# A two-block transformer on one core: first modulation's products written ahead of the norm, rope tables and gates behind the first dense block

## The chip, the cores and the metric

The kernel runs on one core of a Trainium2 chip. The metric is the device time of one execution in microseconds; three executions of the kernel before are given, and one more was taken with a profile.

## What is computed

`reference()` runs two blocks over 256 tokens of width 1024, all in fp32. The change lies in the opening of the first block:

```python
def first_block(x, c, positions, w_ada, b_ada, norm1_g, w_in, b_gate, conv_w, ...):
    mod = jax.nn.silu(c) @ w_ada[l] + b_ada[l]          # 1024 -> 6 * 1024
    sh1, sc1, g1, sh2, sc2, g2 = jnp.split(mod, 6, axis=-1)
    h = rms_norm(x, norm1_g[l]) * (1.0 + sc1[:, None, :]) + sh1[:, None, :]
    proj = h @ w_in[l]
    q_a, k_a, v_a, qk_m, v_m, o_m, gates = jnp.split(proj, offs, axis=-1)
    # rope on q_a, k_a and block attention; a causal convolution of width 4 and silu on qk_m;
    # a chunkwise mLSTM whose input and forget gates come from `gates`
    ...
    # output projection, second modulated norm, mixture of 32 experts, residual
```

Behind it come the mixture of experts and a second block (gated linear attention, a state space layer, attention to a memory), which the change does not touch.

## The kernel before, in words

Activations are kept transposed, 128 partitions of the width by 256 tokens, eight slices `k`. A product with a weight is made from two halves of each operand, `hi` and `lo`, by three matmuls (`mm3`, L282 to L286). Weights come in tiles `w` of 1 MB by SyncE's queue (`load`, L254), through a pool of five buffers. `halves` (L271) takes such a tile in two halves of 1024 columns: ScalarE copies each to `whi` (L267), VectorE subtracts to get `wlo` (L268). A dense block of 256 output columns (`dense_t`, L288) is two column tiles, one per half; for each it runs 8 slices by 3 matmuls, so 48 matmuls of 128x256 in all.

`first` (L437) sets the order of the work around the change; the scheduler lets instructions of one engine pass each other only as its priorities and the data allow, and the order on each engine is fixed before the kernel runs.

- The norm: `rstd` (L352) squares eight slices on ScalarE (L324, tile `ats`, two buffers) and sums each by two matmuls with one column (`ps<-c_ident,ats`); a square root and a reciprocal (L333, L334) give `cvc`, two matmuls spread it over the partitions and ScalarE copies it to `cv` (L349). VectorE scales the input with it (L448).
- Rope tables: the positions come by DMA (L450), and VectorE and ScalarE make sine and cosine (L463 to L465, `sincos` L360). The mask constants and the frequencies come by `load_c` (L444), `c_cmask` being one transfer.
- The modulation: `ada` (L404) loads eight 1 MB slices of `wada`, multiplies each with the replicated condition `crep` in four matmuls of 32x512, copies the sum (`ats`, L414), transposes it (L417) and adds a bias (`mod`, L420). The generator yields after each slice. The first third is run through at L467; the other two are kept in `more`, and one step of it is taken behind each later dense block (`next(more)`).
- `hh` and `hl`: the scaled input, modulated, as `hi` on ScalarE (L474) and `lo` on VectorE (L475, L476), slice by slice.
- Gates: `wg` and `bg` come by DMA, eight matmuls make `ml<-s,wg`, and `gates` (L570) takes a sigmoid and a logarithm on ScalarE, running sums on VectorE, transposes (L598) and products that spread them (L280, `ml<-s,c_cmask`).
- Dense blocks: four of them, b = 0, 2, 1, 3 (L488), each followed by one `more` step, a copy to `raw` (L493) and the convolution (L498 to L500).

Of the kernel before, what the change touches and what calls it, by code (L numbers as in the profile page):

```python
# [13 lines left out]
I32 = mybir.dt.int32  # L14
U8 = mybir.dt.uint8
AF = mybir.ActivationFunctionType
OP = mybir.AluOpType
AX = mybir.AxisListType

T = 256  # L20
# [187 lines left out]
class Kern:  # L208
# [86 lines left out]
    def steps_t(self, ps, src, act):  # L295
        for c, w in enumerate(self.halves(src)):
            w = [x.rearrange("p (k m) -> p k m", k=8) for x in w]
            for k in range(8):
                self.mm3(ps[:, c], [x[:, k] for x in w], [x[:, k] for x in act], k == 0, k == 7)
                if k % 4 == 3:  # L300
                    yield

    def dense_n(self, src, act):

        ps = self.psum().rearrange("p (a b) -> p a b", a=2)
        for _ in self.steps_n(ps, src, act):
            pass
        return ps
# [128 lines left out]
    def first(self, M):  # L437
        nc, io, tc = self.nc, self.io, self.tc
        with tc.tile_pool(name="p1", bufs=1) as P, tc.tile_pool(name="p1w", bufs=2) as W:
            sc = self.t(P, [128, 8], "sc")  # L440
            nc.scalar.activation(sc, self.v("c"), AF.Silu)
            crep = self.t(P, [128, 8, 32], "crep")
            nc.vector.tensor_copy(crep, sc[:, :, None].to_broadcast([128, 8, 32]))
            C = self.load_c(P, ["cmask", "tneg", "rot", "hsel", "invf"])  # L444

            r1, _ = self.rstd(W, self.xT, "cv", sq="ats")
            hT = self.slot(0).rearrange("p (a b) -> p a b", a=8)
            nc.vector.tensor_mul(hT, self.xT, bc(r1, 8))  # L448
            posi = self.t(W, [128, T], "cv", I32)
            nc.sync.dma_start(posi, io["pos"].to_broadcast([128, T]))  # L450
            s3, s4, s5, s6 = self.slot(3), self.slot(4), *(self.wx.tile([128, 2048], F32, tag="w", name="w") for _ in range(2))
            ao = s3[:, 0:1024].rearrange("p (a h d) -> p a h d", a=2, h=8)
            so = s3[:, 1024:].rearrange("p (f t) -> p f t", f=4)
# [1 line left out]
            t1 = s4[:, 1024:1536].rearrange("p (a t) -> p a t", a=2)  # L455
            sinT, cosT = s4[:, 1536:1792], s4[:, 1792:]
# [2 lines left out]
            mE = itertools.cycle([s5[:, 1584 + 128 * i:1712 + 128 * i] for i in range(2)])  # L459
            pT0, raws = (itertools.cycle([s6[:, o + 512 * i:o + 512 * i + 512].rearrange("p (a t) -> p a t", a=2) for i in range(2)])  # L460
                         for o in (0, 1024))
            ang = t1[:, 0]
            nc.vector.tensor_copy(ang, posi)  # L463
            nc.vector.tensor_scalar(ang, ang, C["invf"], None, op0=OP.mult)
            self.sincos(P, ang, T, "rp", (W, "cv"), (sinT, cosT))  # L465
            for _ in self.ada(W, 0, crep):
                pass  # L467
            more = itertools.chain(self.ada(W, 1, crep), self.ada(W, 2, crep))
            a1 = self.t(P, [128, 8], "a1")
            nc.vector.scalar_tensor_tensor(a1, self.m(1), 1.0, self.v("norm1_g"), op0=OP.add, op1=OP.mult)  # L470
# [5 lines left out]
                nc.vector.tensor_sub(hl[:, k], hT[:, k], hh[:, k].bitcast(F32))  # L476
            h = (hh, hl)
            self.out("h", hT)
            wg = self.t(P, [128, 8, 36], "wg")
            nc.sync.dma_start(wg, io["wgate"][0])  # L480
            bg = self.t(P, [36, 1], "bg")
# [5 lines left out]

            qkm = self.slot(1).rearrange("p (a b) -> p a b", a=8)  # L488
            for b in (0, 2, 1, 3):
                ps = self.dense_t(io["win"][4 + b], h)  # L490
                next(more, None)
                raw = next(raws)
                nc.scalar.activation(raw, ps, AF.Copy)  # L493
                for c in range(2):
                    f = 2 * b + c
                    cv = qkm[:, f]
                    wc = self.v("conv_w", 4 * f, 4)
                    nc.vector.tensor_scalar(cv, raw[:, c], wc[:, 3:4], self.v("conv_b", f), op0=OP.mult, op1=OP.add)  # L498
                    for d in (1, 2, 3):
                        nc.vector.scalar_tensor_tensor(cv[:, d:], raw[:, c, :T - d], wc[:, 3 - d:4 - d], cv[:, d:],  # L500
                                                       op0=OP.mult, op1=OP.add)
                if b >= 2:
                    for x in (qkm[:, 2 * b - 4:2 * b - 2], qkm[:, 2 * b:2 * b + 2]):
                        nc.scalar.activation(x, x, AF.Silu)
                    nc.gpsimd.tensor_scalar(x, x, 128.0 ** -0.5, None, op0=OP.mult)
            nc.vector.memset(vm[:, :, :, 128:132], 1.0)
            for b in range(2):
                ps = self.dense_n(io["winv"][2 + b], h)
# [8 lines left out]
            for b in range(2):  # L517
                for s, o in enumerate((qT, kT)):
                    ps = self.dense_t(io["win"][2 * s + b], h)
# [8 lines left out]
                ps = self.dense_n(io["winv"][b], h)  # L528
# [8 lines left out]
            for b in range(2):  # L537
                ps = self.dense_t(io["win"][8 + b], h)
# [30 lines left out]

    def gates(self, P, C, pg, bg, hn, so):  # L570

# [1270 lines left out]
```

## Time and profile before

| | |
|---|---|
| time, median of 3 runs | 1500.61 us (1500.07 to 1500.84) |
| the profiled execution | 1499.36 us |
| its span in the trace | 1497.3 us |
| TensorE busy | 1337.9 us, 89% |
| VectorE, ScalarE, GpSimd busy | 51%, 37%, 22% |
| mean granted TensorE clock | 0.93 |
| DMA, mean over the span | 277 GB/s |

The time of an execution is a little more than the span of its trace, by what lies around the first and last instruction. The span counts from the first to the last of them. PE is TensorE's matmuls, PEld its weight loads, which overlap with matmuls; DVE is VectorE, ACT ScalarE, POOL GpSimd, SP SyncE. In the timeline, a row is one or several neighbouring instructions of one form; the brackets give the idle time of the engine before it and the releaser inferred for it. A busy share is a mean over stages with different limits.

### The profile page before, as it was taken

Reading aid. Unit: us, or ns where it says so; the run is one execution under the profiler, and the core shown is the slowest. Engines: PE = TensorE matmul, PEld = TensorE weight load, DVE = VectorE, ACT = ScalarE, POOL = GpSimd, SP = SyncE. Lnnn points to the kernel's source line nnn. Section 1 sums busy time; section 2 is a strip of 40 time slices with the busy share of each in tenths; the row PEclk is TensorE's granted clock in tenths of the full one; section 3 lists DMA queues with packets and bytes.
Section 4 is the critical chain, followed back from the end, with each engine's and each line's share of the span. In section 5 each row is a group of like instructions: output and inputs, shape, how many; then the busy total and the mean of one; then the engine's idle time right before and its main releaser. Section 6 shows DMA issues by size and latency. Waiting matters only on the chain. (4 is left out here: it accounts for less than half of the span.)

```text
span 1497.3 us, 25797 instructions
## 1 busy us (share of the span) xinstructions
PE 1337.9 (89%) x10632; PEld 1065.1 (71%) x10632; DVE 761.6 (51%) x1498; ACT 549.8 (37%) x859; POOL 323.3 (22%) x450
## 2 busy tenths in 40 slices
PE   5999998987887888686679999999999999999997
PEld 2777796553454555341159989999888988999997
DVE  2766454812233321010047686588846899665553
ACT  3754553321211122110034435644522355444443
POOL 0031121412223231200008887111400000030001
PEclk8899999998988999896689999999999999999998
DMA  9776764999999999999994525889766534675540
GB/s 364 277 268 250 268 246 174 379 400 420 420 408 415 420 408 420 420 421 374 421 370 156 204 92 178 259 251 320 265 203 204 170 138 147 213 205 189 178 141 29
DMA packets 87626, 414.86 MB, mean 277 GB/s; under 512 B 26432, under 2 KB 28016, under 8 KB 43472
## 3 DMA queue, kind: packets, MB, share of 16 engines
q1 hardware_dynamic: 66768, 381.85, 66.9%
q0 software_dynamic: 8016, 22.13, 4.7%
q10 hardware_dynamic: 12720, 9.18, 1.9%
q8 instruction: 86, 1.41, 0.4%
q14 instruction: 36, 0.29, 0.1%
HBM read 392.90 MB, written 20.22 MB: 276 GB/s over the span
## 5 line engine op out<-in xcount | busy, mean ns | idle before, releaser
L267 ACT ACTIVATE whi<-w 128x1024 fp32r<-128x1024 f32 x252 | 263.7, 1056 | 329.8 <-PE ps L280 249.9
L268 DVE TENSOR_TENSOR wlo<-w,whi 128x1024 fp32r<-128x1024 f32 x222 | 273.4, 1240 | 145.2 <-ACT whi L267 144.6
L280 PE MATMUL ps<-hh,whi 128*128 128x256 f32 x928 | 272.8, 294 | 11.2 <-DVE zt L1614 5.0
L280 PE MATMUL ps<-hh,wlo 128*128 128x256 f32 x928 | 266.9, 288 | 2.0 <-DVE wlo L268 1.8
L280 PE MATMUL ps<-hl,whi 128*128 128x256 f32 x928 | 267.8, 289 | 0.9 <-DVE hl L1579 0.7
L280 PEld LDWEIGHTS ps<-hh,whi 128*128 128x128 f32 x928 | 179.0, 193 | 19.5 <-issue 9.1
L280 PEld LDWEIGHTS ps<-hh,wlo 128*128 128x128 f32 x928 | 178.8, 193 | 4.5 <-DVE wlo L268 2.6
L280 PEld LDWEIGHTS ps<-hl,whi 128*128 128x128 f32 x928 | 179.0, 193 | 2.0 <-DVE hl L1579 0.7
L280 PE MATMUL A<-w,xg 128*32 128x512 f32 x984 | 139.6, 667 | 33.8 <-DMA w<-in_w 32.9
L280 PE MATMUL acc<-gyl,whi 128*128 128x256 f32 x384 | 109.1, 284 | 0.6 <-DVE gyl L268 0.6
L280 PE MATMUL acc<-gyh,wlo 128*128 128x256 f32 x384 | 109.1, 284 | 0.0
L280 PE MATMUL acc<-gyh,whi 128*128 128x256 f32 x384 | 108.2, 282 | 0.0
L268 POOL TENSOR_TENSOR wlo<-w,whi 128x1024 fp32r<-128x1024 f32 x30 | 70.6, 2368 | 167.1 <-ACT whi L267 166.9
L934 DVE SCALAR_TENSOR_TENSOR xT<-m,mod,xT 128x256 f32<-128x256 f32 x64 | 27.8, 480 | 142.7 <-PE m L280 142.7
L280 PEld LDWEIGHTS A<-w,xg 128*32 128x32 f32 x984 | 23.8, 114 | 102.3 <-DMA w<-in_w 73.2
L280 PE MATMUL A<-w,gT 128*32 128x512 f32 x512 | 75.0, 687 | 24.1 <-DMA w<-in_w 16.5
L960 DVE TENSOR_TENSOR g<-g,A 128x512 f32<-128x512 f32 x8 | 5.5, 687 | 134.3 <-PE A L280 134.3
L280 PEld LDWEIGHTS acc<-gyl,whi 128*128 128x128 f32 x384 | 72.7, 189 | 1.5 <-DVE gyl L268 0.8
L280 PEld LDWEIGHTS acc<-gyh,whi 128*128 128x128 f32 x384 | 73.2, 191 | 0.2 <-issue 0.2
L280 PEld LDWEIGHTS acc<-gyh,wlo 128*128 128x128 f32 x384 | 72.9, 190 | 0.2 <-issue 0.2
L1759 POOL TENSOR_TENSOR zs<-zs,yy 128x256 f32<-128x256 f32 x16 | 14.7, 935 | 236.9 <-DMA yy<-yd 236.1
L280 PE MATMUL ps<-wlo,hh 128*128 128x256 f32 x192 | 56.1, 292 | 3.4 <-DVE wlo L268 3.4
(585 smaller groups left out, 2766.8 us busy)
## 6 DMA issues: line engine op xcount, KB each, us to landing
w<-in_w SPq DMA_DIRECT2D x187, 1024.0 KB, 11.5
w<-in_wada SPq DMA_DIRECT2D x24, 1024.0 KB, 7.3
w<-in_wo SPq DMA_DIRECT2D x24, 1024.0 KB, 5.3
w<-in_sglu SPq DMA_DIRECT2D x16, 1024.0 KB, 4.9
w<-in_gz SPq DMA_DIRECT2D x12, 1024.0 KB, 6.9
w<-in_sz SPq DMA_DIRECT2D x12, 1024.0 KB, 4.8
w<-in_win SPq DMA_DIRECT2D x10, 1024.0 KB, 7.1
w<-in_xk SPq DMA_DIRECT2D x8, 1024.0 KB, 9.7
```

The costliest lines, as they stand in the source:

```text
L267: self.nc.scalar.activation(hi, src, AF.Copy)
L268: (eng or self.nc.vector).tensor_sub(lo, src, hi.bitcast(F32))
L280: self.nc.tensor.matmul(ps, l, r, start=start, stop=stop, **kw)
L934: self.nc.vector.scalar_tensor_tensor(self.xT[:, f], pc[:, T * c:T * c + T], self.m(5)[:, f:f + 1], self.xT[:, f], op0=OP.mult, op1=OP.add)
L960: nc.vector.tensor_mul(g1, g1, p3)
L1759: nc.gpsimd.tensor_mul(zs[:, f], zs[:, f], u)
```

## The change

`ada` 0 is written ahead of the norm. A new `dense_k` makes a block of 256 columns with the slices outside and its two column tiles inside, so that both halves of the weights are in use from the first slice; it makes block 0 (`ahead`), straight behind `hh` and `hl`. The constants, the positions, the rope tables, the gate weights, the gate products and `gates` stand behind it in the program. The loop over the blocks takes `ahead` for b = 0.

```diff
--- before.py
+++ after.py
@@ -300,6 +300,15 @@
                 if k % 4 == 3:
                     yield
 
+    def dense_k(self, src, act):
+        ps = self.psum().rearrange("p (a b) -> p a b", a=2)
+        w = [[x.rearrange("p (k m) -> p k m", k=8) for x in y] for y in self.halves(src)]
+        for k in range(8):
+            for c in range(2):
+                self.mm3(ps[:, c], [x[:, k] for x in w[c]], [x[:, k] for x in act], k + c == 0, k + c == 8, skip_group_check=True)
+        return ps
+
     def dense_n(self, src, act):
 
         ps = self.psum().rearrange("p (a b) -> p a b", a=2)
@@ -441,13 +450,12 @@
             nc.scalar.activation(sc, self.v("c"), AF.Silu)
             crep = self.t(P, [128, 8, 32], "crep")
             nc.vector.tensor_copy(crep, sc[:, :, None].to_broadcast([128, 8, 32]))
-            C = self.load_c(P, ["cmask", "tneg", "rot", "hsel", "invf"])
+            for _ in self.ada(W, 0, crep):
+                pass
 
             r1, _ = self.rstd(W, self.xT, "cv", sq="ats")
             hT = self.slot(0).rearrange("p (a b) -> p a b", a=8)
             nc.vector.tensor_mul(hT, self.xT, bc(r1, 8))
-            posi = self.t(W, [128, T], "cv", I32)
-            nc.sync.dma_start(posi, io["pos"].to_broadcast([128, T]))
             s3, s4, s5, s6 = self.slot(3), self.slot(4), *(self.wx.tile([128, 2048], F32, tag="w", name="w") for _ in range(2))
             ao = s3[:, 0:1024].rearrange("p (a h d) -> p a h d", a=2, h=8)
             so = s3[:, 1024:].rearrange("p (f t) -> p f t", f=4)
@@ -459,12 +467,6 @@
             mE = itertools.cycle([s5[:, 1584 + 128 * i:1712 + 128 * i] for i in range(2)])
             pT0, raws = (itertools.cycle([s6[:, o + 512 * i:o + 512 * i + 512].rearrange("p (a t) -> p a t", a=2) for i in range(2)])
                          for o in (0, 1024))
-            ang = t1[:, 0]
-            nc.vector.tensor_copy(ang, posi)
-            nc.vector.tensor_scalar(ang, ang, C["invf"], None, op0=OP.mult)
-            self.sincos(P, ang, T, "rp", (W, "cv"), (sinT, cosT))
-            for _ in self.ada(W, 0, crep):
-                pass
             more = itertools.chain(self.ada(W, 1, crep), self.ada(W, 2, crep))
             a1 = self.t(P, [128, 8], "a1")
             nc.vector.scalar_tensor_tensor(a1, self.m(1), 1.0, self.v("norm1_g"), op0=OP.add, op1=OP.mult)
@@ -476,6 +478,15 @@
                 nc.vector.tensor_sub(hl[:, k], hT[:, k], hh[:, k].bitcast(F32))
             h = (hh, hl)
             self.out("h", hT)
+            ahead = self.dense_k(io["win"][4], h)
+            C = self.load_c(P, ["cmask", "tneg", "rot", "hsel", "invf"])
+
+            posi = self.t(W, [128, T], "cv", I32)
+            nc.sync.dma_start(posi, io["pos"].to_broadcast([128, T]))
+            ang = t1[:, 0]
+            nc.vector.tensor_copy(ang, posi)
+            nc.vector.tensor_scalar(ang, ang, C["invf"], None, op0=OP.mult)
+            self.sincos(P, ang, T, "rp", (W, "cv"), (sinT, cosT))
             wg = self.t(P, [128, 8, 36], "wg")
             nc.sync.dma_start(wg, io["wgate"][0])
             bg = self.t(P, [36, 1], "bg")
@@ -487,7 +498,7 @@
 
             qkm = self.slot(1).rearrange("p (a b) -> p a b", a=8)
             for b in (0, 2, 1, 3):
-                ps = self.dense_t(io["win"][4 + b], h)
+                ps = self.dense_t(io["win"][4 + b], h) if b else ahead
                 next(more, None)
                 raw = next(raws)
                 nc.scalar.activation(raw, ps, AF.Copy)
```

In the changed program the lines are: modulation copy L423, its transposes L426, `mod` L429; squares L333, root L342, spreading L358; scaling L458; `hh` L476, `hl` L477 and L478; rope tables L378 to L387, L487 and L488; gates L586 to L627 (transposes L609); `raw` L504, convolution L509 and L511, silu L515.

The first place is ScalarE at the start of the program, behind the condition's silu. Before (`ats<-xT` are the norm's squares, `ats<-ps` the modulation's copy, `s_156` the tables):

```order
L324 ACTIVATE ats<-xT 128x256 x8
L333 ACT_TABLE_LOAD
L333 ACTIVATE cvc<-ps,c_ident 128x2
L349 ACTIVATE cv<-ps 128x256
L376 ACT_TABLE_LOAD
L376 ACTIVATE s_156<-cv 128x256
L378 ACTIVATE s_156<-cv,c_ident 128x256
L414 ACTIVATE ats<-ps 128x512
L474 ACTIVATE hh<-s_151,mod,a_229 128x256 x8
L267 ACTIVATE whi<-w 128x1024 x4
```

Now:

```order
L423 ACTIVATE ats<-ps 128x512
L333 ACTIVATE ats<-xT 128x256 x8
L267 ACTIVATE whi<-w 128x1024
L342 ACT_TABLE_LOAD
L342 ACTIVATE cvc<-ps,c_ident 128x2
L267 ACTIVATE whi<-w 128x1024
L358 ACTIVATE cv<-ps 128x256
L476 ACTIVATE hh<-s_206,mod,a_212 128x256 x8
L267 ACTIVATE whi<-w 128x1024 x3
```

The copy that ends the modulation comes first, then the eight squares; two of the weight splits of block 0 stand inside the norm, and sine and cosine are no longer in front of `hh`.

The second place is TensorE at the start. Before, in the order of its queue:

```order
L280 MATMUL ps<-c_ident,ats 128x1 x16
L280 MATMUL ps<-c_ident,cvc 128x128 x2
L280 MATMUL ps<-w,crep 32x512 x32
L417 MATMUL ps<-c_ident,ats 128x128 x4
L280 MATMUL ml<-s_151,wg 36x256 x7
L280 MATMUL ps<-hh,whi 128x256
```

Now:

```order
L280 MATMUL ps<-w,crep 32x512 x32
L426 MATMUL ps<-c_ident,ats 128x128 x4
L280 MATMUL ps<-c_ident,ats 128x1 x16
L280 MATMUL ps<-c_ident,cvc 128x128 x2
L280 MATMUL ps<-hh,whi 128x256
L280 MATMUL ps<-w,crep 32x512
L280 MATMUL ps<-hl,whi 128x256
```

The 32 products of the modulation go in front of the sums, and the gate products no longer stand in front of the block.

The third place is TensorE around the gate chain's transposes (L598 before, L609 now; `ml<-c_ident`). Before, inside the second block:

```order
L280 MATMUL ps<-w,crep 32x512 x4
L280 MATMUL ps<-hh,whi 128x256
L598 MATMUL ml<-c_ident,s_156 128x4
L280 MATMUL ps<-hl,whi 128x256
L598 MATMUL ml<-c_ident,s_156 128x4
L280 MATMUL ps<-hh,wlo 128x256
```

Now, from the last matmul of the second block to the first ones of the third:

```order
L280 MATMUL ps<-hh,wlo 128x256
L280 MATMUL ps<-w,crep 32x512 x5
L609 MATMUL ml<-c_ident,s_209 128x4 x2
L280 MATMUL ps<-w,crep 32x512 x4
L280 MATMUL ps<-hh,whi 128x256
L280 MATMUL ml<-s_208,c_cmask 128x256 x2
L280 MATMUL ps<-hl,whi 128x256
```

The first two transposes, and the products that spread the gates behind them, moved from inside the second block to the stretch between the second and the third, with the third queued behind them.

VectorE's queue ahead of those transposes now reads, from the last step of the rope tables on (`s_209` are tables and gates, `s_369` the convolution):

```order
L386 SCALAR_TENSOR_TENSOR cv<-cv 128x256
L586 TENSOR_SCALAR s_209<-ml,bg 4x256
L587 TENSOR_SCALAR s_209<-ml,bg 4x256
L511 SCALAR_TENSOR_TENSOR s_369<-w,vec,s_369 128x253
L588 SCALAR_TENSOR_TENSOR s_209<-s_209 4x256
L509 TENSOR_SCALAR s_369<-w,vec 128x256
L591 TENSOR_SCALAR s_209<-s_209 4x256
L511 SCALAR_TENSOR_TENSOR s_369<-w,vec,s_369 128x255
L268 TENSOR_TENSOR wlo<-w,whi 128x1024
L511 SCALAR_TENSOR_TENSOR s_369<-w,vec,s_369 128x254
L511 SCALAR_TENSOR_TENSOR s_369<-w,vec,s_369 128x253
L268 TENSOR_TENSOR wlo<-w,whi 128x1024
L592 TENSOR_TENSOR s_209<-s_209 4x256
```

The gate steps (L586 to L592), which before stood between the weight splits of the first blocks, now stand between the convolution of block 0 and the splits of the third block.

## Rows read from the trace of the kernel before

**Rows 1.** The page's first part: busy time of each engine, its share of the span, and the number of instructions.

```profile
PE 1337.9 (89%) x10632; PEld 1065.1 (71%) x10632; DVE 761.6 (51%) x1498; ACT 549.8 (37%) x859; POOL 323.3 (22%) x450
```

**Rows 2.** Timeline of TensorE (PE matmuls, PEld weight loads) from 0 to 42 us: start, duration, engine, line, operation, out<-in, shapes, count; in brackets the idle time before and what ended it.

```profile
8.23 6.99 PE L280 MATMUL ps<-c_ident,ats 128*128 128x1 f32 x32 [8.23 <-ACT ats L324]
...
17.01 5.69 PE L280 MATMUL ps<-w,crep 128*32 128x512 f32 x32
...
21.24 0.12 PEld L280 LDWEIGHTS ps<-w,crep 128*32 128x32 f32 x4 [0.62 <-DMA w<-in_wada]
...
23.20 1.06 PE L280 MATMUL ps<-w,crep 128*32 128x512 f32 x8 [0.51 <-DMA w<-in_wada]
...
30.81 1.94 PE L280 MATMUL ps<-w,crep 128*32 128x512 f32 x8 [0.55 <-DMA w<-in_wada]
33.52 1.12 PE L417 MATMUL ps<-c_ident,ats 128*128 128x128 f32 x4 [0.78 <-ACT ats L414]
36.19 5.91 PE L280 MATMUL ml<-s,wg 128*36 128x256 f32 x14 [1.55 <-DVE s L475]
```

**Rows 3.** Timeline of VectorE (DVE), same columns, 17 to 74 us.

```profile
17.53 2.29 DVE L448 TENSOR_TENSOR s<-xT,cv 128x2048 f32<-128x2048 f32 x1 [1.73 <-ACT cv L349]
...
20.06 0.35 DVE L464 TENSOR_SCALAR s<-s,c_cmask 128x256 f32<-128x256 f32 x1
...
22.81 0.43 DVE L377 SCALAR_TENSOR_TENSOR cv<-cv 128x256 f32<-128x256 f32 x1
...
35.72 0.41 DVE L475 TENSOR_SCALAR s<-s,a,mod 128x256 f32<-128x256 f32 x1 [0.67 <-ACT hh L474]
...
40.78 1.21 DVE L268 TENSOR_TENSOR wlo<-w,whi 128x1024 fp32r<-128x1024 f32 x1
41.92 0.41 DVE L476 TENSOR_TENSOR hl<-s,hh 128x256 fp32r<-128x256 f32 x1
...
71.41 2.45 DVE L500 SCALAR_TENSOR_TENSOR s<-w,vec,s 128x255 f32<-128x255 f32 x6
```

**Rows 4.** Timeline of ScalarE (ACT), same columns, 13 to 43 us.

```profile
13.61 0.42 ACT L324 ACTIVATE ats<-xT 128x256 f32<-128x256 f32 x1 [0.44 <-PE ps L280]
14.04 1.28 ACT L333 ACT_TABLE_LOAD   x1
15.34 0.26 ACT L333 ACTIVATE cvc<-ps,c_ident 128x2 f32<-128x2 f32 x1
...
32.87 0.60 ACT L414 ACTIVATE ats<-ps 128x512 f32<-128x512 f32 x1 [9.09 <-PE ps L280]
35.08 4.05 ACT L474 ACTIVATE hh<-s,mod,a 128x256 fp32r<-128x256 f32 x8 [1.62 <-DVE a L470]
39.04 3.88 ACT L267 ACTIVATE whi<-w 128x1024 fp32r<-128x1024 f32 x4
```

**Rows 5.** TensorE's weight loads that read the squares of a norm against `c_ident`, in the first norm and in the last one of the program: count, shortest/median/longest in ns, first and last start in us.

```profile
L280 PEld LDWEIGHTS ps<-c_ident,ats x32: 288/333/338, 8.2 to 14.8; 128*128 128x128 f32 x32
...
L280 PEld LDWEIGHTS st<-c_ident,yy x32: 192/192/338, 1482.8 to 1486.9; 128*128 128x128 f32 x32
```

**Rows 6.** Stretches of the first stage: window in us, its length, busy us (and count) of PE, PEld, DVE, ACT and POOL, PEclk (share of the full TensorE clock), share of the DMA engines, GB/s.

```profile
15.00:20.00 5.00, 4.37 (x22) 1.86 (x25) 2.64 (x3) 2.26 (x4) 0.00 (x0) 1.00 1.00 423
30.00:35.00 5.00, 3.31 (x16) 0.92 (x12) 0.29 (x2) 0.60 (x1) 0.00 (x0) 0.50 0.99 407
100.00:110.00 10.00, 7.82 (x55) 5.91 (x54) 6.28 (x15) 6.19 (x14) 9.37 (x12) 1.00 0.53 203
110.00:130.00 20.00, 17.83 (x134) 15.26 (x133) 16.72 (x39) 10.89 (x24) 4.42 (x6) 1.00 0.66 236
```

**Rows 7.** DMA issues: queue and count, KB of one, us from issue to landing.

```profile
c_cmask<-in_cst SPq DMA_DIRECT2D x1, 512.5 KB, 6.9
```

**Rows 8.** Single microseconds of the first loads, columns as in the stretches.

```profile
12.00:13.00 1.00, 1.00 (x7) 1.00 (x6) 0.00 (x0) 0.56 (x2) 0.00 (x0) 1.00 0.42 109
13.00:14.00 1.00, 1.00 (x6) 1.00 (x6) 0.00 (x0) 0.56 (x2) 0.00 (x0) 1.00 0.56 159
```

**Rows 9.** Timeline of TensorE from 49 to 79 us.

```profile
49.37 0.28 PE L280 MATMUL ps<-hh,wlo 128*128 128x256 f32 x1
...
56.07 1.91 PE L280 MATMUL ml<-s,c_cmask 4*128 4x256 f32 x12
...
59.12 0.41 PE L280 MATMUL ps<-hh,whi 128*128 128x256 f32 x1
...
62.10 0.31 PE L280 MATMUL ps<-hh,wlo 128*128 128x256 f32 x1
...
64.19 0.39 PE L280 MATMUL ps<-hh,whi 128*128 128x256 f32 x1
...
69.81 0.28 PE L280 MATMUL ps<-hh,wlo 128*128 128x256 f32 x1
...
76.97 1.90 PE L280 MATMUL ps<-w,crep 128*32 128x512 f32 x10
```

**Rows 10.** Timeline of TensorE among the loads of the experts' weights.

```profile
351.34 1.51 PE L280 MATMUL A<-w,gT 128*32 128x512 f32 x8 [0.55 <-DMA w<-in_w]
...
407.94 1.06 PE L280 MATMUL A<-w,xg 128*32 128x512 f32 x8 [1.95 <-DMA w<-in_w]
...
410.76 1.94 PE L280 MATMUL A<-w,xg 128*32 128x512 f32 x8 [1.76 <-DMA w<-in_w]
```


## The prediction

> **What bounds the kernel now.** I read the page first: TensorE is busy 89% of the span [rows 1]. Then stretches of 5 us, which show where that share has other meanings: the instruction streams of the two programs differ only in what before ran from 0 to about 130 us, so only that stage is costed, and what it loses or gains is carried to the end. Behind it the streams are the same, and the big weight stream starts when the stage's consumers free its buffers, so it shifts too. Then the timelines of the stage, engine by engine, in order of time: what ends last.
>
> Before, the modulation's 8 MB set the start. The last group of its products begins at 30.81 when its load has landed, runs 1.94 and ends at 32.75 [rows 2]. The norm costs nothing: its sums run from 8.23 to 15.22 and its scaling ends by 19.8 [rows 2, 3], all under the loads. From 32.75 it is 2.33 us to the first `hh` at 35.08 [rows 4].
>
> The clock must be read from durations here. The window from 15 to 20 us prints 1.00 [rows 6], but the square sums' weight loads take a median of 333 ns, against 192 in the last norm [rows 5]. So TensorE starts at 1.2 GHz. The products begun at 17.01 load their weights at a faster step only from 21.24 [rows 2]. From 30 to 35 us the row says 0.50 again [rows 6].
>
> **The change, step by step.** The times are those of the profiled execution (1499.36 us, 1.25 under the median of 1500.61), as lag against before. Order rows give the sequence.
>
> *1. The modulation ends earlier.* The mask constants (512.5 KB, [rows 7]) and the positions (128 KB by their shape) no longer go ahead of the last load: 640.5 KB at 423 GB/s [rows 6] is 1.55 us. TensorE now frees buffers as loads land, so I also take out the hole at 12 to 14 us, where 109 and 159 GB/s moved [rows 8]: 0.58 MB short, 1.37 us. The end, T, is at 32.75 - 2.9 = 29.85. Bounds: 31.2 if the hole stays, 28.95 if the last group also takes 1.06 (as at 23.20, [rows 2]) instead of 1.94.
>
> *2. The norm now stands behind it.* ScalarE's stream has the modulation's copy ahead of the squares, so none of the squares can start before T. From T, by rows of before: copy 0.7 with its wait, transposes 1.12, sums 6.99 [rows 2, 4]. Squares keep step with the sums, two buffers deep; the last one ends 1.2 us before them (13.61 + 0.42 against 15.22), at T + 7.6. Then a weight split moved ahead 1.04 (half of two, from four in 3.88), table load 1.28 [rows 4], and from the square root to the start of the scaling, over the reciprocal and its spreading, 2.19 (15.34 to 17.53, [rows 3, 4]): T + 12.1. The second split half of VectorE, released by ScalarE's second, ends about T + 12.5; the scaling takes 2.2 [rows 3]: T + 14.7. First `hh` at 44.5, before 35.08: **lag 9.4**. The table load and the sums were hidden by the loads; that cover is gone.
>
> *3. First dense block.* VectorE starts 0.64 us behind `hh` and needs 5.5 for 16 instructions (35.72 to 42.33, without the split between) plus a cast of 0.3: last `hl` at 50.9 [rows 3]. Both tiles follow it piece by piece, so PE could end at 51.6. But the clock is probably low then, after a norm that leaves TensorE half idle; the products from 17.01 came to the faster step only 4.2 us later [rows 2]. I carry that over as an estimate: 20 products at 0.213, the step of the slow ones (14 from 59.12 to 62.10, [rows 9]), then 28 at 0.117 (64.19 to 69.81 for 48, [rows 9]): 45.6 to 53.2. Before: 49.37 + 0.28 = 49.65. **Lag 3.5**: most of step 2 comes back, as the splits lie ahead.
>
> *4. Gate products and second block.* Eight gate products used to run under the making of `hh` (36.19, 14 records in 5.91, [rows 2], at the lower clock). Now they stand behind the block: 16 records at half of 0.42, 3.4 us; with three modulation products 0.65. Second block, 48 products at 0.117: 57.3 to 62.9; before it ended at 62.4, since it held the gate chain's products and a stretch at the slow step (59.12 to 62.10, [rows 9]). **Lag 0.5**, but with the gate chain outstanding.
>
> *5. The gate chain becomes a wait.* Five modulation products bring PE to 64.0. Next in its queue are two transposes of the gate rows, and the third block is queued behind them. VectorE must first do, behind the last `hl`: the rest of the rope tables 3.2 (20.06 to 23.24), five splits at 1.14 (40.78 to 41.92, 5.7), eight convolution steps 3.1 (2.45 for six and two short ones), and ten short instructions of the gates, an estimate of 3.0 from the 0.35 and 0.43 of the tables' own [rows 3]: 14.9 us, so 65.8. PE waits 1.8. Then transposes 0.5, four modulation products 0.9, the chain's products 3.3 (1.91 for the larger set, [rows 9]; the rest an estimate at the same step) and the block 5.6: third block ends at 76.1, before at 69.81 + 0.28 [rows 9]; one modulation product more is done. **Lag 5.8**. This step is the least certain: ScalarE's sine, exponential and logarithm with their table loads (1.28 each, [rows 4]) stand in that chain too, and each one late is a longer wait.
>
> *6. To the end of the stage.* Before lost 0.8 at 76.97, where ten records took 1.90 [rows 9]; with the loads ahead I expect that back: **lag 5.0**. The moved transfers themselves (constants, positions, gate weights) cost nothing there: they are queued while TensorE is busy with blocks, and are needed 20 us later. If that cover failed, they cost the 1.55 us again.
>
> Sum: 1500.61 + 5.0 = 1505.6. By bounds of the terms, about 1500 (every clock term at its better end) to 1510.
>
> **Clock: rows and rule.** Among the expert loads the same kind of product comes in groups with waits between: one took 1.06 after an idle of 1.95, the next 1.94 after 1.76, and another 1.51, part at the faster step [rows 10]. So a fed group may meet either level, and I take the lower at T. The Trainium skill, "TensorE: Matmul & The Clock Gate", section on HAM oscillation, says that a group of products shorter than the wait for its next slice lets the clock fall, so that each group starts slow; that speaks against writing products ahead, paced by loads. By that rule alone T would be 29.85 as in step 1; the rows allow 28.95, since they also show a group that gained speed.
>
> **Rivals.**
> A. *The clock holds at 2.4 GHz through the norm.* Then T is 28.95 and the sums are paced by ScalarE, 8 times 0.43 instead of 6.99: 4.4 less, lag 0.6, 1501.2. It decides from the level at T. For it: eight groups at short distance lie ahead. Against it: sums of this kind did nothing for the clock from 8.23 to 15.22. If half of it holds: 1503.4.
> B. *Not slower, by slack behind.* TensorE idles 2.18 of 10 us at 100 to 110 and 2.17 of 20 at 110 to 130 [rows 6], waiting for VectorE's recurrent part. If that part's vector work is then ready before a later PE, up to 4.35 comes back: lag 0.65, 1501.3. Against it: VectorE itself is later by the rope tables and its place in the gate chain. A and B together: 1496.9, faster.
> C. *The wait of step 5 lets the clock fall.* Then the 48 products of the third block take 0.213 each, 4.6 more: 1510.2. It decides where the wait is long enough for the granted clock to drop; before showed such a slow stretch at 59 to 62 inside the second block.
> That the change doesn't do what it says is no rival: the order rows show it on all engines.
>
> **How the numbers follow.** Forecast 0.44, A (or half of it) 0.25, B 0.10, C 0.12, A with B 0.09. A measurement tells about 0.2%, 3.0 us, from no change. Slower by more: C, nearly all of the forecast and a little of A, 0.52; within: the rest of A, B and a corner of the forecast, 0.38; faster: most of A with B and a little of A and B, 0.10. The range from 1499.0 to 1509.5 leaves out A with B and most of C, 0.17. The forecast's own, by its terms' bounds without rivals, is 1502.5 to 1508.5.
>
> **What would show it.** In the profile after: the copy of the modulation near 30 instead of 32.87; squares behind it at steps of 0.85 (0.43 if A holds); first `hh` near 44; the block's products in sixes, ending near 53; a TensorE idle in front of the gate transposes near 64 to 66; the third block's end near 76. Wrong if `hh` comes before 41, if no idle stands in front of the transposes, or if the lag at 76 is gone by 130.

## The result, and the profile after

The changed kernel takes 1516.09 us, median of six runs (1512.29 to 1519.62), against 1500.72 (1496.62 to 1503.91, six runs) before: a ratio of 1.0105, interval 1.0083 to 1.0127, about 15.4 us slower. The forecast was slower, but 1505.6 in a range of 1499.0 to 1509.5: the direction held, the size did not. The profiled execution took 1519.36, near the slowest of the six, with a span of 1517.3. Its first part answers to [rows 1]: TensorE was busy 7.2 us longer with the same 10632 matmuls, the other engines' busy times hardly moved, and the rest of the 20 us is waiting:

```profile
PE 1345.1 (89%) x10632; PEld 1068.6 (70%) x10632; DVE 762.8 (50%) x1498; ACT 550.8 (36%) x860; POOL 322.8 (21%) x450
```

TensorE's timeline from 10 to 66 us (start, duration, engine, line, operation, shapes, count, in brackets the idle time before and what ended it) answers to [rows 2, 9]:

```profile
10.05 1.94 PE L280 MATMUL ps<-w,crep 128*32 128x512 f32 x8 [10.05 <-DMA w<-in_wada]
12.44 1.85 PE L280 MATMUL ps<-w,crep 128*32 128x512 f32 x8 [0.46 <-DMA w<-in_wada]
14.92 1.06 PE L280 MATMUL ps<-w,crep 128*32 128x512 f32 x8 [0.64 <-DMA w<-in_wada]
17.41 1.91 PE L280 MATMUL ps<-w,crep 128*32 128x512 f32 x8 [1.42 <-DMA w<-in_wada]
...
27.35 1.62 PE L280 MATMUL ps<-w,crep 128*32 128x512 f32 x8 [1.42 <-DMA w<-in_wada]
29.67 1.12 PE L426 MATMUL ps<-c_ident,ats 128*128 128x128 f32 x4 [0.70 <-ACT ats L423]
30.58 6.91 PE L280 MATMUL ps<-c_ident,ats 128*128 128x1 f32 x32
...
52.69 0.28 PE L280 MATMUL ps<-hh,wlo 128*128 128x256 f32 x1
...
63.35 1.90 PE L280 MATMUL ps<-w,crep 128*32 128x512 f32 x10
65.18 0.28 PE L609 MATMUL ml<-c_ident,s 4*128 4x4 f32 x2
65.40 1.06 PE L280 MATMUL ps<-w,crep 128*32 128x512 f32 x8
```

The modulation ends at 27.35 + 1.62 = 28.97 instead of 32.75. The norm's sums then take 6.91, at the slow step, with nothing beside them. The first block ends at 52.69 + 0.28 = 52.97. ScalarE in the same place, and where the fourth block's copy is made (answers to [rows 4]):

```profile
29.02 0.60 ACT L423 ACTIVATE ats<-ps 128x512 f32<-128x512 f32 x1 [25.62 <-PE ps L280]
...
30.89 0.42 ACT L333 ACTIVATE ats<-xT 128x256 f32<-128x256 f32 x1 [0.97 <-PE ps L426]
...
37.26 1.28 ACT L342 ACT_TABLE_LOAD   x1
...
43.26 4.04 ACT L476 ACTIVATE hh<-s,mod,a 128x256 fp32r<-128x256 f32 x8 [2.48 <-DVE s L458]
...
85.68 1.28 ACT L708 ACT_TABLE_LOAD   x1 [0.24 <-DVE qs L710]
86.97 0.40 ACT L708 ACTIVATE wi<-Mb,mprev 128x128 f32<-128x128 f32 x1
87.28 0.58 ACT L504 ACTIVATE w<-ps 128x512 f32<-128x512 f32 x1
```

The modulation's copy is at 29.02, the squares follow. The second square waits 0.97 for the transposes of that copy: copy and squares share the two `ats` buffers. First `hh` is at 43.26, 8.2 later than the 35.08 of before. Further on, TensorE from 72 to 88 us:

```profile
72.52 0.41 PE L280 MATMUL ps<-hh,whi 128*128 128x256 f32 x1
...
75.08 0.41 PE L280 MATMUL ps<-hh,whi 128*128 128x256 f32 x1
...
77.50 1.92 PE L280 MATMUL ps<-w,crep 128*32 128x512 f32 x14
...
85.30 1.06 PE L280 MATMUL ps<-w,crep 128*32 128x512 f32 x8
87.91 0.39 PE L280 MATMUL ps<-whi,hh 128*128 128x256 f32 x1 [1.55 <-ACT w L504]
```

and from 121 to 126 us:

```profile
121.91 0.81 PE L280 MATMUL ml<-w,mS 128*128 128x132 f32 x2 [5.20 <-DVE mS L704]
...
123.17 0.42 PE L280 MATMUL ps<-hl,whi 128*128 128x256 f32 x1
...
125.73 0.41 PE L280 MATMUL ps<-hl,whi 128*128 128x256 f32 x1
```

The 5.20 of idle at 121.91 has no answer in the groups ahead of the prediction. What ended it is VectorE, whose `mS` stands behind the rope sum of the attention's first block (second row; the first row is the gate chain, for the account of step 5), and behind VectorE is GpSimd, whose rows around the cosine product (L537) are these:

```profile
64.56 0.46 DVE L599 TENSOR_TENSOR s<-s 4x128 f32<-4x128 f32 x2
...
120.90 0.69 DVE L538 TENSOR_TENSOR s<-s,w 128x512 f32<-128x512 f32 x1 [5.54 <-POOL w L537]
```

```profile
118.92 0.72 POOL L1098 TENSOR_TENSOR kvo<-kvo 128x256 f32<-128x256 f32 x1
119.60 1.26 POOL L537 TENSOR_TENSOR w<-w,s 128x512 f32<-128x512 f32 x1
```

The same place in the kernel before, where that product is L526, and the waits of VectorE and of TensorE behind it:

```profile
104.20 0.73 POOL L1087 TENSOR_TENSOR kvo<-kvo 128x256 f32<-128x256 f32 x1
104.89 1.28 POOL L526 TENSOR_TENSOR w<-w,s 128x512 f32<-128x512 f32 x1
106.14 0.60 POOL L1086 TENSOR_TENSOR kvo<-w 128x256 f32<-128x256 f32 x1
```

```profile
106.21 1.08 DVE L527 TENSOR_TENSOR s<-s,w 128x512 f32<-128x512 f32 x1 [1.35 <-POOL w L526]
```

```profile
108.34 0.49 PE L280 MATMUL ml<-w,mS 128*128 128x132 f32 x2 [1.90 <-DVE mS L693]
```

Before, the cosine product stood behind the squares of four of the memory's eight slices; it started at 104.89, VectorE waited 1.35 for it and TensorE 1.90. Now all eight slices stand ahead of it on GpSimd, whose order is fixed before the kernel runs, and their load has landed later too (the first square starts at 107.30, before at 99.11): the product starts only at 119.60, and VectorE idles 5.54 for it.

To carry a lateness through the program I use one row that all kernels have: the last transposes of the modulation, near the end of the stage. Before and after:

```profile
186.07 0.60 PE L417 MATMUL ps<-c_ident,ats 128*128 128x128 f32 x4
```

```profile
199.96 0.60 PE L426 MATMUL ps<-c_ident,ats 128*128 128x128 f32 x4
```

So the **stage lag** is 13.9. What lies behind the stage makes it 20.1 at the program's end in this execution; over the runs it is 15.4, so most of the loss is the stage's, if the lag of this one trace holds for the other runs.

### The profile page after: what moved, and what is told of

Its sections match the earlier page's. It is cut to its first block, busy times and chain, and to the rows that moved or that the text cites. A ratio compares the mean times of both kernels' runs of the same rounds, so it can differ in the third digit from the quotient of the medians.

```text
span 1517.3 us, 25801 instructions
## 1 busy us (share of the span) xinstructions
PE 1345.1 (89%) x10632; PEld 1068.6 (70%) x10632; DVE 762.8 (50%) x1498; ACT 550.8 (36%) x860; POOL 322.8 (21%) x450
## 5 line engine op out<-in xcount | busy, mean ns | idle before, releaser
L280 PE MATMUL A<-w,xg 128*32 128x512 f32 x984 | 142.7, 681 | 32.5 <-DMA w<-in_w 31.7
L280 PE MATMUL A<-w,gT 128*32 128x512 f32 x512 | 76.6, 696 | 23.6 <-DMA w<-in_w 15.2
```

Of the source, the lines that this page charges most:

```text
L280: self.nc.tensor.matmul(ps, l, r, start=start, stop=stop, **kw)
```

## The experiments

All twelve are edits of the kernel before (B) or of the changed one (A). Stage lag is the start of those transposes minus 186.07; it comes from one trace of each kernel, and e7 below shows that two traces can differ by 1.6 to 2 in the opening alone. The kernel before was timed beside each group of runs, at medians of 1501.0 to 1501.9.

| run | edit | stage lag | median us | ratio to before, interval |
|---|---|---|---|---|
| e1 | A, cosine products on VectorE | 8.6 | 1515.33 | 1.0114 (1.0081 to 1.0147) |
| e2 | A, memory norm behind the attention's loop | 14.5 | 1516.74 | 1.0105 (1.0075 to 1.0135) |
| e3 | A, norm first again | 2.3 | 1503.71 | 1.0020 (1.0004 to 1.0036) |
| e4 | B, modulation ahead, nothing else | 18.6 | 1521.44 | 1.0141 (1.0109 to 1.0172) |
| e5 | A, first half of cosine products on VectorE | 9.1 | 1513.72 | 1.0089 (1.0056 to 1.0122) |
| e6 | A, norm between the modulation's slices | 0.7 | 1500.87 | 0.9997 (0.9975 to 1.0018) |
| e7 | B, both tiles side by side, nothing else | 0.5 | 1505.38 | 1.0038 (1.0013 to 1.0064) |
| e8 | B, norm between the slices | -1.7 | 1500.93 | 0.9998 (0.9975 to 1.0020) |
| e9 | A, memory load and norm ahead of the loop | 7.9 | 1508.52 | 1.0046 (1.0025 to 1.0067) |
| e10 | e8 with the memory early | -0.2 | 1499.00 | 0.9988 (0.9973 to 1.0003) |
| e11 | e8 with e5's products | -2.3 | 1500.66 | 1.0006 (0.9985 to 1.0027) |
| e12 | e6 with e9 | -0.3 | 1499.42 | 0.9986 (0.9971 to 1.0001) |

**GpSimd's queue: e1, e5, e2, e9.** In e1 (and in e5 for `b == 0` alone):

```diff
-                    nc.gpsimd.tensor_mul(raw, raw, bc(cosT, 2))
+                    nc.vector.tensor_mul(raw, raw, bc(cosT, 2))
```

> The changed kernel, with the product of the raw block and the cosine table (L537) on VectorE instead of GpSimd. Theory (GpSimd's queue: that product stands behind all 15 squares and sums of the memory norm, and VectorE and TensorE wait for it 5.5 and 5.2 us at 115 to 122 us): the idle before the state product near 121 us goes, with the slow products behind it 6.5 us in all, less some 1.5 of added vector work; the lag at the first vector instruction of the attention's mask (13.8 in the changed kernel) falls to 8 to 10, the time from 1516.1 to 1509 to 1512. Rival (the lateness comes from the opening, and the wait at 121 only shows it): the lag stays at 13 to 14, the time within 2 of 1516.

```profile
194.63 0.60 PE L426 MATMUL ps<-c_ident,ats 128*128 128x128 f32 x4
```

The stage did what the theory said: 194.63 - 186.07 = 8.6, inside 8 to 10, and the wait of 5.20 is gone. The time did not: 1515.33 is hardly under 1516.09, and it is the time that the rival gave. The lag in the trace was 5.9 behind the place of the wait and 8.6 only after the second half, which VectorE now did as well; so the next run left that half on GpSimd.

> The changed kernel, with the cosine product on VectorE in the first half of the attention's blocks only; the second half stays on GpSimd. Theory (GpSimd's queue costs some 8 at 122 us; the 2.4 that the run with all four on VectorE lost again behind 150 us was VectorE's added work): lag 5.5 to 6.5 from 122 us to the end of the stage instead of 13.9. By that the time is 1507 to 1511; if the stage shows it and the time stays above 1513, the rest is lost behind the stage, where TensorE's granted clock stays low for shorter or longer behind the routing. Rival (opening alone): lag 13 to 14.

The lag was 9.9 ahead of the place of the wait and 8.9 behind it, where in the changed kernel it rose from 9.0 to 13.9; it then stayed at 8.9 to 9.1. The bound of 6.5 was missed, since this execution came 1 us later out of the first blocks. The time, 1513.72, again lost less than the stage.

In e2 the call of `self.memory(M)` moved from the end of the attention's first pass to behind the loop:

```diff
-                if b == 0:
-                    self.memory(M)
+            self.memory(M)
             for b in range(2):
                 ps = self.dense_t(io["win"][8 + b], h)
```

> The changed kernel, with the memory norm's first part written behind the attention's loop instead of inside it, so that the product with the cosine table is the first of the two in GpSimd's queue; no engine has more work. Theory (GpSimd's queue): as with the product on VectorE, lag 8 to 9 instead of 13.8 at the attention's first mask, time 1509 to 1511. Rival (opening): lag 13 to 14, 1514 to 1518. The 1 MB of the memory is loaded later, which by itself should cost under 1.

GpSimd, and TensorE at the place that then waited:

```profile
111.06 1.29 POOL L537 TENSOR_TENSOR w<-w,s 128x512 f32<-128x512 f32 x1 [17.80 <-PE ps L280]
...
146.18 1.28 POOL L537 TENSOR_TENSOR w<-w,s 128x512 f32<-128x512 f32 x1
```

```profile
153.54 0.47 PE L652 MATMUL at<-c_ident,ats 128*128 128x128 f32 x1 [5.08 <-ACT ats L648]
```

The first cosine product is early now (111.06), and the lag fell to 3.1 at 122 to 140 us. But the second pass has the same product, and that one (146.18) now stands behind the memory's products; VectorE waits 2.03 for it and 2.56 for GpSimd's product of L664, and both stand between the memory's products; TensorE idles 5.08 at 153.54, and the lag is back at 14.5. Lag and time are those of the rival and the forecast of 8 to 9 failed; but the lag had been down to 3.1, and the wait moved with the memory's products, which fits the theory. So e9 put `self.memory(M)` ahead of the loop:

```diff
+            self.memory(M)
             for b in range(2):
                 for s, o in enumerate((qT, kT)):
...
                 if b == 0:
-                    self.memory(M)
```

> The changed kernel, with the memory's load and first part of its norm written ahead of the attention's loop: GpSimd is through with it before the cosine product is due, and no engine has more work. Theory (GpSimd's queue, not the opening alone, makes the last 5 of the 13.9 in the stage): no idle of over 2 before the state product near 122 us, lag 7.5 to 10 from there on, time 1508 to 1513. Rival (another wait takes its place, as where the memory norm stood behind the loop; here it could be the scaling of the mLSTM's keys, which now stands behind the memory's products on GpSimd): lag 12 or more. The two runs with the cosine product on VectorE lost less time than their traces say (13.7 to 15 over the kernel before, with 9 in the stage); if that repeats, it lies behind the stage.

```profile
96.91 0.80 POOL L1098 TENSOR_TENSOR kvo<-kvo 128x256 f32<-128x256 f32 x1
...
115.83 1.29 POOL L538 TENSOR_TENSOR w<-w,s 128x512 f32<-128x512 f32 x1 [16.50 <-PE ps L280]
```

```profile
193.96 0.60 PE L426 MATMUL ps<-c_ident,ats 128*128 128x128 f32 x4
```

GpSimd is through with the memory at 97.71 and takes the cosine product at 115.83. The keys' scaling that the rival named is late: it starts behind the memory's products at 97.79, and the lag is 11.3 where the changed kernel has 9.0. That comes back around the first cosine product, for which no engine waits now: 10.7 at 115.6 us, 8.6 at 117.0. Stage lag 7.9, time 1508.52: both as expected. This run has no more work on any engine than the changed kernel, and 6 of its 13.9 in the stage and 7.6 of its time are gone. Between e9's time and those of e1 and e5, with nearly the same stage, 5 to 7 us stay unexplained; by subtraction they lie behind the stage.

**The norm behind the modulation: e3, e4, e6.** e3 puts the first modulation behind the norm again and keeps the rest of the change; e4 does the reverse in the kernel before, where the two lines go from behind the tables to behind `load_c`. The edit of e3:

```diff
-            for _ in self.ada(W, 0, crep):
-                pass
             r1, _ = self.rstd(W, self.xT, "cv", sq="ats")
...
+            for _ in self.ada(W, 0, crep):
+                pass
             more = itertools.chain(self.ada(W, 1, crep), self.ada(W, 2, crep))
```

> The changed kernel, with the first modulation written behind the norm again; the block with both tiles, the tables and the gates behind it stay as changed. Theory (the norm behind the modulation costs 8 us at the first hh): first hh at 33 to 35, first block ends at 45 to 48, so 2 to 5 earlier than before; GpSimd's queue has the cosine product behind six of the memory norm's eight pairs, so part of the wait near 115 stays. Time 1497 to 1503. Rival (tables and gates behind the block carry the loss): gate chain late as in the change, 1508 or more.

```profile
34.94 4.04 ACT L476 ACTIVATE hh<-s,mod,a 128x256 fp32r<-128x256 f32 x8 [1.62 <-DVE a L472]
```

First `hh` is at 34.94 again, and 1503.71 is 12.4 under the changed kernel, a little over the bound of 1503. The first block was expected to end at 45 to 48 and ended at 50.60; of the eight slices of the memory norm six stand ahead of the cosine product, and the stage lag is 2.3.

> The kernel before, with the first modulation written ahead of the norm and nothing else. Theory (the norm behind the modulation, and GpSimd's order, carry the loss): first hh at 43 to 45, and GpSimd has the cosine product behind the whole memory norm again; time 1508 to 1518. Rival (the moved tables and gates carry it): 1500 to 1505.

```profile
44.58 4.04 ACT L474 ACTIVATE hh<-s,mod,a 128x256 fp32r<-128x256 f32 x8 [1.54 <-DVE s L450]
```

```profile
126.88 0.81 PE L280 MATMUL ml<-w,mS 128*128 128x132 f32 x2 [5.18 <-DVE mS L693]
```

Worse than the whole change: `hh` at 44.58, the wait for GpSimd again (5.18 at 126.88), 1521.44 against an expected 1508 to 1518. So the moved tables and gates, with both tiles side by side, do not carry the loss; once the modulation is ahead they give back about 5. The time lies above the expected range.

e6 keeps the modulation ahead and writes the norm behind its third slice:

```diff
+            first = self.ada(W, 0, crep)
+            for _ in range(3):
+                next(first)
-            for _ in self.ada(W, 0, crep):
-                pass
             r1, _ = self.rstd(W, self.xT, "cv", sq="ats")
             hT = self.slot(0).rearrange("p (a b) -> p a b", a=8)
             nc.vector.tensor_mul(hT, self.xT, bc(r1, 8))
+            for _ in first:
+                pass
```

> The changed kernel, with the norm written behind the third of the modulation's eight slices, so that products of the first slices, the norm's sums and the other slices alternate on TensorE; everything else stays as changed. Theory (what costs is the norm standing behind the whole modulation, not the modulation standing ahead of it): squares and sums run under the loads, the modulation's copy comes at 29 to 31 and the first hh at 31.5 to 33.5, before the 35.08 of the kernel before; time 1497 to 1503. Rival (the early modulation disturbs the loads or the clock whatever the norm does): hh behind 35, 1505 or more.

TensorE at the start of e6, and its first `hh` on ScalarE:

```profile
10.30 1.94 PE L280 MATMUL ps<-w,crep 128*32 128x512 f32 x8 [10.30 <-DMA w<-in_wada]
12.17 2.72 PE L280 MATMUL ps<-c_ident,ats 128*128 128x1 f32 x12
14.82 1.93 PE L280 MATMUL ps<-w,crep 128*32 128x512 f32 x8
...
30.36 1.06 PE L280 MATMUL ps<-w,crep 128*32 128x512 f32 x8 [1.42 <-DMA w<-in_wada]
```

```profile
33.30 4.04 ACT L478 ACTIVATE hh<-s,mod,a 128x256 fp32r<-128x256 f32 x8 [1.16 <-DVE a L474]
```

Products and sums alternate and the sums lie under the loads again: first `hh` at 33.30, 10 earlier than in the changed kernel. Against before it is 1.8 earlier, but e7, which has no edit ahead of `hh`, has it at 33.00. The modulation's copy, at 31.55, missed its bound of 31. On GpSimd six slices still stand ahead of the cosine product, and the lag grows there from -2.1 to 0.7. Time 1500.87: the loss of 15 is gone with the modulation's first products still in front.

**The rest of the change, and better versions: e7, e8, e10 to e12.** e7 has the new block alone, with `dense_k` as in the change and nothing moved:

```diff
             self.out("h", hT)
+            ahead = self.dense_k(io["win"][4], h)
...
-                ps = self.dense_t(io["win"][4 + b], h)
+                ps = self.dense_t(io["win"][4 + b], h) if b else ahead
```

> The kernel before, with its first block made by the new function (both column tiles side by side) and nothing moved. Theory (this part is nearly free: the block ends when the last slice of the activation and the four weight halves are there): time 1499 to 1504, lag at the end of the stage -3 to 3. Rival (both tiles wait for the second half of the weights, which before came while the first tile ran): first block 2 to 4 later, 1504 or more.

The stage lag of 0.5 agrees with the theory; the time, 1505.38, is 1.4 over its bound and where the rival had it. The rival's reason does not show: the first block ends at 48.26, 15.26 behind the first `hh`, against 14.57 before, so 0.7 later and not 2 to 4. What the time has over the kernel before is not seen in the stage and stays open. The modulation ended at 31.12 with no edit in front of it, 1.6 before the kernel before, and the first `hh` came at 33.00, 2.1 before: so much a single trace may differ at that place.

e8 is e6's norm in the kernel before, with the constants behind the modulation:

```diff
-            C = self.load_c(P, ["cmask", "tneg", "rot", "hsel", "invf"])
+            first = self.ada(W, 0, crep)
+            for _ in range(3):
+                next(first)
             r1, _ = self.rstd(W, self.xT, "cv", sq="ats")
             hT = self.slot(0).rearrange("p (a b) -> p a b", a=8)
             nc.vector.tensor_mul(hT, self.xT, bc(r1, 8))
+            for _ in first:
+                pass
+            C = self.load_c(P, ["cmask", "tneg", "rot", "hsel", "invf"])
...
-            for _ in self.ada(W, 0, crep):
-                pass
```

> The kernel before, with the norm written behind the third slice of the modulation and the mask constants and positions loaded behind the modulation's slices; block, tables and gates as before. Theory: first hh at 31.5 to 33.5 instead of 35.08, one or two of these microseconds lost again to the tables, which now wait for their constants and share VectorE with hl; lag at the end of the stage -4 to 0, time 1497 to 1502. Rival (no gain, since the weights of the first block land no earlier): lag 0 to 2.

Stage lag -1.7 as expected, time 1500.93, no difference. e10 adds to e8 the edit of e9, e11 that of e5, and e12 is e6 with the edit of e9.

> The kernel before, with the norm between the modulation's slices (lag -1.7 at the end of the stage when run alone) and the memory's load and products ahead of the attention's loop. Theory: the 2.2 that TensorE idles at 105 to 110 us behind GpSimd's product go too; lag -3 to -6 at 130 us, time 1495 to 1499. Rival (the idle has another cause, or the early memory load delays the loads of the blocks by its 2.5): lag -2 to 1, 1499 to 1503.

The stage lag is -0.2, as the rival had it: the early memory gave nothing there, and the 1.5 behind e8 is within what single traces differ. The time, 1499.00, is not told apart from before.

> The kernel before, with the norm between the modulation's slices and the first half's cosine products on VectorE. Theory: as with the memory early, the wait for GpSimd goes, less some 1.4 of added vector work: lag -2 to -4 at 130 us, time 1496 to 1500. Rival (VectorE is the bound there): lag -1.7 to 1, 1500 to 1503.

Stage lag -2.3 as expected; the time, 1500.66, is in the rival's range: again nothing that the time shows.

> The changed kernel with both causes mended: the norm between the modulation's slices (0.7 at the end of the stage by itself, -2.3 before the wait for GpSimd) and the memory's load and products ahead of the attention's loop. Theory (the two are separate): lag -3 to 0 at 130 us, time 1497 to 1501. Rival (they share a cause, so the second mends nothing more, or the scaling of the keys on GpSimd is late instead): lag 0.5 to 4, 1501 to 1505.

```profile
185.78 0.60 PE L426 MATMUL ps<-c_ident,ats 128*128 128x128 f32 x4
```

With both causes mended the changed kernel stands at -0.3 in the stage and 1499.42, 16.7 under the change. Mending the two takes the whole loss away; e6, with the norm alone mended, had already done so in time (1500.87), and the two are not told apart. Nor do the gains add: alone they are 15.2 (e6) and 7.6 (e9), together 16.7. So the norm written behind the whole modulation is the cause without which little or nothing is lost (e3, e6), and GpSimd's queue makes its loss larger. Against the kernel before neither e10 nor e12 is a gain beyond the interval (0.9971 to 1.0001 for e12).

## Why the prediction was right in direction and wrong in size

- *Step 1.* The modulation ended at 28.97, near the better bound (28.95) rather than at 29.85, and by luck: the last group took 1.62, not the 1.06 of that bound, but began at 27.35, half a microsecond before the load was forecast to land.
- *Step 2 held.* Squares behind the copy, sums at the slow step, table load and scaling: first `hh` at 43.26, lag 8.2 (forecast 9.4). Rival A, the faster clock through the norm, did not come: the sums took 6.91 against 6.99 before, and the granted clock reads 0.50 from 30 to 40 us. e3, e4 and e6 show that this serial norm is where the loss starts.
- *Steps 3 and 4 held in their sums.* First block to 52.97 (forecast 53.2), second to 63.14 + 0.28 = 63.4 (62.9); lags 3.3 and 1.0. In step 3 two errors offset: only some 10 products went at the slow step, not 20, but one modulation product at that step (1.92, at 44.42) stood among them, which the sum had left out.
- *Step 5 held in place, not in mechanism.* No idle stands in front of the gate transposes, which the prediction had named as a sign of being wrong: VectorE's chain was done at 65.02 and they ran at 65.18. TensorE came there later than the 64.0 of the forecast, since the five modulation products took 1.83, not 1.1: four of them run side by side (eight records in 1.06, at 65.40) and a fifth alone takes nearly as long as four (ten records in 1.90, at 63.35). That is still 0.6 before the 65.8 of the forecast; what came late is the stretch from there to the end of the third block, 12.4 where the sum had 10.3. The third block had some 15 products at the slow step (13 from 72.52 to 75.08, 0.213 apart, and those at the ends), a third of rival C: 1.5 more; the other 0.6 was not traced. The next row begins at 77.50, before at 70.02: lag 7.5, forecast 5.8.
- *Step 6 failed, first half.* I read the 1.90 of ten records at 76.97 [rows 9] as 0.8 lost that would come back. It is the same fifth product alone: nothing was lost there. Instead seven products now stand where four did (1.92 at 77.50), 0.9 more, and at 87.91 TensorE waits 1.55 for ScalarE's copy of the fourth block, which stands behind a table load and an exponential of the mLSTM (85.68, 86.97). Lag 9.0 instead of 5.0: 1.7 from step 5, 0.9, the 0.7 by which that wait is longer than the fifth product was, and the 0.8.
- *Step 6 failed, second half, and this is the step that broke the range.* It carried the lag unchanged from 77 us to the end of the stage and put no cost on GpSimd at all. But GpSimd's queue changed too: its cosine product moved behind the last four slices of the memory norm. That is a lag of 9.0 (at 102 us) turned into 13.9: 5.20 of idle where before there were 1.90, and behind it 13 products at 0.213 instead of 0.117 (123.17 to 125.73), 4.6 together; shorter waits ahead of it add 1.2 and nearly as much comes back behind. Rival B put slack at this place, the opposite of what came. e9 shows it: the same kernel with the memory's work out of the way ends the stage at 7.9 and the program at 1508.52, inside the range that was given. The first half alone, a lag of 9.0, would have come to 1509.7 (1500.7 + 9.0, an estimate by lag alone), at the edge of the range.
- *Behind the stage.* Over the runs 1.5 of the 15.4 would lie there, in the profiled execution 6.2. The largest piece can be seen: both kernels idle some 5 us for the router (250 us after, 236 before). Before, TensorE was soon back at 2.4 GHz; after, it stayed at 1.2 GHz for the whole rows from 250 to 265, busy nearly throughout, and the stretch from the end of the idle to the first expert product took 19.78 against 13.96: 5.8 of the 6.2. The changed kernel first (the row from 120 belongs to the wait above; columns: window, length, busy us and count of PE, PEld, DVE, ACT, POOL, then PEclk, DMA share, GB/s), then the one before:

```profile
120.00:130.00 10.00, 8.09 (x50) 8.09 (x51) 6.84 (x23) 2.86 (x8) 0.86 (x1) 0.66 0.47 143
240.00:250.00 10.00, 5.15 (x43) 4.95 (x42) 9.32 (x19) 5.51 (x10) 5.77 (x4) 0.98 0.31 106
250.00:260.00 10.00, 9.59 (x45) 9.62 (x46) 4.46 (x31) 0.48 (x2) 0.00 (x0) 0.50 0.43 133
260.00:265.00 5.00, 5.00 (x28) 4.74 (x28) 1.15 (x2) 1.65 (x4) 0.00 (x0) 0.50 0.00 0
```

```profile
227.00:237.00 10.00, 4.69 (x37) 4.52 (x36) 9.52 (x24) 4.62 (x7) 4.75 (x3) 0.96 0.39 116
237.00:247.00 10.00, 10.00 (x79) 9.73 (x79) 5.54 (x29) 2.72 (x8) 0.00 (x0) 0.87 0.35 123
```

Why one execution recovers sooner than another was not settled. It is not why e1 and e7 stand above what their stages say: in their traces the same stretch is 14.26 and 14.03, only in e5's is it longer (16.37). Behind the stage the profiled executions differ from the kernel before by -3.4 (e9) to 6.8 (e7), and single runs of the kernel before spread over more than 10; the cause of that spread stays open.

*Clock: rows and rule.* The changed kernel's modulation is eight equal groups, 2.49 apart, each done before the next load has landed. Their durations were 1.94, 1.85, 1.06, 1.91, 1.54, 1.06, 1.07 and 1.62: both levels, in no fixed turn. The Trainium skill, "TensorE: Matmul & The Clock Gate", section "HAM oscillation — how this bites in real kernels", says of groups that are shorter than the wait for their next slice that the clock falls in the wait and the next group starts slow; its example has waits of about 3 to 5 us behind about 2 us of products. The trace bears that out only in part: three groups here were shorter than the wait behind them (1.06 or 1.07, then 1.42 of idle), and the next ones took 1.91, 1.07 and 1.62, one slow, one fast, one of both; and the second group, at 1.85, was nearly all slow behind a wait of only 0.46.

## What to carry to other kernels

A step that is written earlier pushes what stood there behind it: ask what was hidden under the waits of the moved step (here a norm under 8 MB of loads) and put it between the parts rather than behind the whole. Compare the order of every engine, GpSimd too: with the edit, bulk work of a later stage came in front of one short product on the critical chain, and the lag grew there by 4.9 of 13.9. Why the scheduler chose that order was not shown; in e3 and e6, where the opening is not late, it still put six slices there instead of four. A lag is not a constant to be carried forward; each engine that has spare work to slip in ahead can make it grow.

## What the runs showed of the hardware that was not expected

Four products of 32x512 into the four groups of 32 output rows of one tile ran side by side: eight records took 1.06, as long as the two records of a single product (1.05, at 42.45 in the kernel before), while a fifth brought ten records to 1.90. After an idle of 5.20, 13 products of 128x256 went at 0.213 instead of 0.117 each, so that wait cost 1.3 more than it lasted; in the window from 120 to 130 us the granted clock reads 0.66. After an idle of 5.26 at the router TensorE was busy 14.6 of the 15 us from 250 to 265 and the granted clock read 0.50 throughout; in the kernel before, after 5.31 of idle, it read 0.66 from 235 to 240 us and 1.00 from 240 to 245.
